# A two-layer hybrid decoder step: the samples' cache pages on three queues, groups of quarter products, and a wider operand in the compression

## Chip, core and metric

The kernel runs on one core of one Trainium2 chip. The metric is the device time of one launch in microseconds (us), the median of a few runs. One more execution was recorded by the hardware profiler; all rows below come from it.

## What is computed

A prompt of 512 tokens and 8 samples of one token each pass through two decoder layers with shared weights: half a feed-forward block, a token mixer of three branches (a state-space scan, sparse attention, a short convolution), half a feed-forward block, each followed by a layer norm. The change lies in the sparse attention of the samples. Each sample has 2048 past rows in 16 pages of 128 rows, found through a page table:

```python
def gather_pages(pool, layer, page_table):
    g = pool[layer, page_table]
...
past_cmp = gather_pages(past['cmp'], layer, past['page_table'])   # compression branch
past_sel = gather_pages(past['sel'], layer, past['page_table'])   # selection branch
...
h = jax.nn.gelu(h_a[:, :-1] + h_b[:, 1:] + h_pe)                  # nsa_compress: first layer
return h @ w2                                                     # second layer
...
kc = partial_rope(kc, c_end)
...
s_s = jnp.einsum('btkgd,btknsd->btkgns', qg, ks_sel)              # nsa_core: scores of the selected blocks
p_s = masked_softmax(s_s.reshape(flat), m_s.reshape(flat))
o_s = jnp.einsum('btkgm,btkmd->btkgd', p_s.astype(vsb.dtype), ...)
s_w = jnp.einsum('btkgd,bwkd->btkgw', qg, kw)                     # window branch
o = g[..., 0:1] * o_c + g[..., 1:2] * o_s + g[..., 2:3] * o_w
```

Compression turns every 32 raw rows into one key and one value by a two-layer network with a GELU; the scores on these choose 16 blocks of 64 rows; attention runs over the chosen blocks and over a window of 512 rows, and gates mix the three results.

## The kernel before

Within a layer the mixer's phases follow one another. During the layer norm ahead of the mixer and the projection of keys, values and queries (`project_kvq`, weights from `w_in`, loaded as `raw` by L218, split by ScalarE into `whi`, L228, and by VectorE into `wlo`, L229) the first pages are fetched. Then two strands are woven into one instruction stream per engine: `compress_cache` (the cached pages of the compression branch, sample by sample, `b` = 0 to 7) and `samples` (the attention of two samples at a time, group `g` = 0 to 3). The last group is woven with the prompt's own attention instead. Each strand is a generator that yields the length of its next wait; a planner picks which strand writes its next piece, and each engine executes what it was given strictly in that order.

The compression's first layer takes eight steps of 12 products per sample (L708, operand `xc`). ScalarE writes the operand's high part (L693, `xc` from `raw` or `cx`) and VectorE the low part (L694), two steps at a time lying ready: while TensorE multiplies one, the other is prepared. The second layer (`second`) takes the two GELUs from ScalarE (L730, `hc`), then four products with 64-column operands (L736: `w2` and the rotated `w2r`, for two key heads each, two instructions per product), two more for the values (L740), and VectorE applies the rotary factors.

A group's pages lie in four tiles `sg`, one for each sample `j` and each half `z` of its 16 pages: 8 pages of 128 KB in a tile, keys in the first 128 columns of a page, values in the others. `fetch_sel` fills them tile by tile: three pages (`NG` = 3) by an indirect transfer that GpSimd (POOL) issues (L1111), five by SyncE (SP), which reads the page numbers from the table into registers (TENSOR_LOAD, L628) and issues a transfer for each (L1115). The group's window rows follow on SP (L1120), then the next pages of the compression. The tiles have one set of buffers: the fetch for group g+1 starts when group g's last product with them (L1242) is done.

The products with pages are quarters: 32 output partitions each, one of TensorE's four column groups for each (z, j). Scores are made in two chunks `c` of four pages, four quarters each (L1182, two instructions per quarter, each 512 columns), in a PSUM bank `S`; then the window's scores (L1191) and those of the samples' own new keys (L1192). The values come in L1242 (pages), L1251 (window), L1255 to L1257 (own new rows and compressed values). The functions that the diff touches, and what calls them:

## Time and profile before

| | |
|---|---|
| median of 3 runs | 3113.18 us (3108.72 to 3114.4) |
| profiled execution | 3112.61 us |
| its span | 3110.9 us |
| mean granted TensorE clock | 0.987 of full speed |
| TensorE busy | 3037.4 us, 98% of the span |
| VectorE, ScalarE, GpSimd busy | 1599.5, 1121.8, 538.6 us |

The span is the stretch of the profiled execution from its first to its last instruction; the execution itself is 1.7 us longer. Busy shares are sums over the whole span. "PE" is TensorE's matmuls, "PEld" its weight loads, "DVE" VectorE, "ACT" ScalarE, "POOL" GpSimd, "SP" SyncE; a q behind an engine's name means its sequencer. The mixer with the samples' attention lies at about 490 to 700 us in the first layer and 2030 to 2245 us in the second.

### The profile page before, as it was taken

What the parts mean: (1) busy time and instruction counts of PE and PEld (TensorE: products, weight loads), DVE (VectorE), ACT (ScalarE), POOL (GpSimd) and SP (SyncE); (2) the same over time, 40 slices, a digit from 0 to 9 for tenths busy, and PEclk for the clock granted to TensorE, in tenths of its full rate; (3) what the DMA queues carried; (4) which work ended last, traced back from release to release, by engine and by line L of the source; (5) the groups of instructions that cost most, each with busy time, mean ns of one, the idle gap of its engine ahead of it and who ended that gap; (6) DMA issues with size and microseconds to landing.
All of it is one profiled execution on the core that took longest, in us unless ns stands there. A gap on an engine that the chain in (4) does not pass through costs nothing. (4 is left out here: it accounts for less than half of the span.)

```text
span 3110.9 us, 62132 instructions
## 1 busy us (share of the span) xinstructions
PE 3037.4 (98%) x25364; PEld 2908.1 (93%) x25364; DVE 1599.5 (51%) x3586; ACT 1121.8 (36%) x2226; POOL 538.6 (17%) x809
## 2 busy tenths in 40 slices
PE   8999999999999999999999999999999999999998
PEld 8999998777999999999999999886779999999998
DVE  7633356566655365333486334564666453743334
ACT  4332235466224233332233322354652342333322
POOL 2611031321001021001257011202210010210010
PEclk9999999999999999999999999999999999999999
DMA  5543254632553232232235332547234433223221
GB/s 158 200 149 128 89 158 137 213 96 59 155 138 105 82 109 82 82 109 85 92 102 171 91 102 89 159 124 216 83 88 134 130 98 97 95 82 100 91 86 64
DMA packets 358630, 360.17 MB, mean 116 GB/s; under 512 B 40068, under 2 KB 341668, under 8 KB 358216
## 3 DMA queue, kind: packets, MB, share of 16 engines
q1 hardware_dynamic: 342584, 333.58, 34.3%
q0 software_dynamic: 7440, 20.00, 2.2%
q8 instruction: 199, 3.26, 0.4%
q10 hardware_dynamic: 8320, 2.62, 0.4%
q14 instruction: 87, 0.71, 0.1%
HBM read 332.48 MB, written 36.28 MB: 119 GB/s over the span
## 5 line engine op out<-in xcount | busy, mean ns | idle before, releaser
L239 PE MATMUL ps<-xh,whi 128*128 128x264 f32 (+1 forms) x4448 | 1258.0, 286 | 14.4 <-ACT whi L228 6.9
L240 PE MATMUL ps<-xl,whi 128*128 128x264 f32 (+1 forms) x4448 | 1258.6, 284 | 2.0 <-DVE xl L323 2.0
L241 PE MATMUL ps<-xh,wlo 128*128 128x264 f32 (+1 forms) x4448 | 1254.8, 284 | 2.4 <-DVE wlo L229 2.4
L229 DVE TENSOR_TENSOR wlo<-raw,whi 128x1024 fp32r<-128x1024 f32 (+3 forms) x432 | 496.0, 1151 | 741.4 <-ACT whi L228 737.3
L239 PEld LDWEIGHTS ps<-xh,whi 128*128 128x128 f32 x4448 | 837.5, 189 | 19.0 <-ACT whi L228 7.7
L240 PEld LDWEIGHTS ps<-xl,whi 128*128 128x128 f32 x4448 | 840.0, 189 | 3.6 <-DVE xl L323 2.2
L241 PEld LDWEIGHTS ps<-xh,wlo 128*128 128x128 f32 x4448 | 839.3, 189 | 4.2 <-DVE wlo L229 3.6
L228 ACT ACTIVATE whi<-raw 128x1024 fp32r<-128x1024 f32 (+2 forms) x452 | 444.5, 988 | 888.4 <-PE ps L240 777.5
L240 PE MATMUL ps<-hl,whi 128*128 128x256 f32 (+1 forms) x1408 | 398.3, 283 | 0.0
L239 PE MATMUL ps<-hh,whi 128*128 128x256 f32 (+1 forms) x1408 | 398.2, 283 | 0.0
L241 PE MATMUL ps<-hh,wlo 128*128 128x256 f32 (+1 forms) x1408 | 398.1, 283 | 0.0
L241 PEld LDWEIGHTS ps<-hh,wlo 128*128 128x128 f32 x1408 | 265.3, 188 | 0.2
L239 PEld LDWEIGHTS ps<-hh,whi 128*128 128x128 f32 x1408 | 264.9, 188 | 0.3
L240 PEld LDWEIGHTS ps<-hl,whi 128*128 128x128 f32 x1408 | 264.8, 188 | 0.1
L260 POOL TENSOR_TENSOR xf<-xf,shift 128x264 f32<-128x264 f32 (+1 forms) x84 | 79.4, 981 | 1027.4 <-ACT shift L257 1027.4
L384 DVE TENSOR_TENSOR s<-s,ps 128x264 f32<-128x264 f32 (+1 forms) x176 | 74.3, 424 | 276.7 <-PE ps L241 276.3
L708 PE MATMUL ps<-xc,whi 128*128 128x256 f32 (+1 forms) x1024 | 166.2, 296 | 0.1
L385 ACT ACTIVATE hh<-s 128x264 fp32r<-128x264 f32 (+1 forms) x176 | 72.7, 415 | 245.1 <-DVE s L384 245.0
L708 PEld LDWEIGHTS ps<-xc,whi 128*128 128x128 f32 x1024 | 141.0, 191 | 14.9 <-issue 8.9
L1111 POOL DMA_INDIRECT sg<-in_selT_dram,idx x96 | 96.5, 1005 | 277.8 <-PE ps L1242 250.7
L382 ACT ACTIVATE s<-ps 128x264 f32<-128x264 f32 (+1 forms) x176 | 66.2, 378 | 128.0 <-PE ps L241 125.6
L386 DVE TENSOR_TENSOR hl<-s,hh 128x264 fp32r<-128x264 f32 (+1 forms) x176 | 76.2, 435 | 33.5 <-ACT hh L385 33.5
(471 smaller groups left out, 4216.3 us busy)
## 6 DMA issues: line engine op xcount, KB each, us to landing
raw<-in_ffn_w_gu_dram SPq DMA_DIRECT2D x86, 1024.0 KB
raw<-in_w_in_dram SPq DMA_DIRECT2D x38, 1024.0 KB
raw<-in_ffn_w_down_dram SPq DMA_DIRECT2D x32, 1024.0 KB
sg<-in_selT_dram SPq DMA_DIRECT2D x160, 128.0 KB
cx<-in_cmpT_dram SPq DMA_DIRECT2D x128, 128.0 KB
raw<-in_cmpT_dram SPq DMA_DIRECT2D x128, 128.0 KB
raw<-in_ffn_w_down_dram SPq DMA_DIRECT2D x16, 768.0 KB
W<-in_winT_dram SPq DMA_DIRECT2D x16, 512.0 KB
```

Source lines behind the costliest of these rows:

```text
L228: self.copy = self.nc.scalar.activation(hi, raw, AF.Copy)
L229: self.lo.tensor_sub(lo, raw, hi.bitcast(F32))
L239: nc.tensor.matmul(o, hi[:, k], rh, start=start and k == 0, stop=False)
L240: nc.tensor.matmul(o, hi[:, k], rl, start=False, stop=False)
L241: nc.tensor.matmul(o, lo[:, k], rh, start=False, stop=stop and k == nk - 1)
L260: nc.gpsimd.tensor_sub(self.xf[:, g, a:b], self.xf[:, g, a:b], sc[:, :n])
L382: nc.scalar.activation(s[:, :n], g, AF.Silu)
L384: nc.vector.tensor_mul(s[:, :n], s[:, :n], u)
L385: nc.scalar.activation(hh[:, j, a:b], s[:, :n], AF.Copy)
L386: nc.vector.tensor_sub(hl[:, j, a:b], s[:, :n], hh[:, j, a:b].bitcast(F32))
L708: nc.tensor.matmul(o, w[:, 2 * qq + q2, :], x[:, 2 * q2:2 * q2 + 2, z:z + n], start=not b and s < 2 and q2 + z + m == 0, stop=s > 5 and q2 ...
L1111: nc.gpsimd.indirect_dma_start(out=t[:, k], out_offset=None, in_=flat, in_offset=bass.IndirectOffsetOnAxis(ap=self.idx[:, l, b, z, k:k + 1 ...
```

## The change

`fetch_sel` works by halves: first the pages 0 to 3 of all four tiles, then the pages 4 to 7. Of four pages POOL fetches one by an indirect transfer (`NG` = 2, one for each half), ScalarE's queue one, and SP two. The page number of ScalarE's page is loaded into a register of ScalarE's. In `samples`, VectorE "opens" each bank by writing one column of zeros (`opened`), the window scores' four quarters stand together ahead of the two small products, and the last six value products are ordered so that both samples' stand side by side. The second layer of the compression takes one 128-column operand `w2k` (`w2` and its rotated copy side by side) for both key heads in one product of 256 columns (two instructions), and VectorE multiplies each head's half by itself.

```diff
-NG = 3
+NG = 2
...
-            nc.vector.tensor_copy(f, self.pt.rearrange("p b (z n) -> p b z n", z=2)[:, :, :, :NG])
+            nc.vector.tensor_copy(f, self.pt.rearrange("p b (z n) -> p b z n", z=2)[:, :, :, ::8 // NG])
...
-    def pages(self, src, l, b, p0, n):
+    def pages(self, src, l, b, p0, n, engine=mybir.EngineType.SP):
...
             pa = self.bank(self.ctp)
-            for j, w in enumerate((self.w2[:, 0], self.w2r)):
-                for kv in range(2):
-                    r = slice(kv * 64, kv * 64 + 64)
-                    nc.tensor.matmul(pa[r, j * 128:j * 128 + 128], w, h[:, kv, :], start=True, stop=True)
...
+            nc.tensor.matmul(pa[:, :256].rearrange("p (k n) -> p k n", k=2), self.w2k, h[:, 0:2, :], start=True, stop=True)
             for kv in range(2):
                 nc.tensor.matmul(pa[:, 256 + kv * 64:256 + kv * 64 + 64], h[:, 2 + kv, :], self.w2[:, 1], start=True, stop=True)
...
-            nc.vector.tensor_mul(t, pa[:, 128:256], self.C["kc_sin"])
-            nc.vector.tensor_mul(kcT, pa[:, :128], self.C["kc_cos"])
+            for kv in range(2):
+                r = slice(kv * 64, kv * 64 + 64)
+                nc.vector.tensor_mul(t[r], pa[64:128, kv * 128:kv * 128 + 128], self.C["kc_sin"][r])
+                nc.vector.tensor_mul(kcT[r], pa[0:64, kv * 128:kv * 128 + 128], self.C["kc_cos"][r])
...
         for z, j in which:
-            b, t = 2 * g + j, pg.tile([128, 8, 256], F32, name="sg")
-            G[z, j] = t
-            for k in range(NG):
+            G[z, j] = pg.tile([128, 8, 256], F32, name="sg")
+
+        for c in range(0, 8, 4):
+            for z, j in which:
+                b, t = 2 * g + j, G[z, j]
                 nc.gpsimd.indirect_dma_start(
-                    out=t[:, k], out_offset=None, in_=flat,
-                    in_offset=bass.IndirectOffsetOnAxis(ap=self.idx[:, l, b, z, k:k + 1], axis=0))
-            for k, s in enumerate(self.pages(src, l, b, 8 * z + NG, 8 - NG)):
-                nc.sync.dma_start(t[:, NG + k], s)
+                    out=t[:, c], out_offset=None, in_=flat,
+                    in_offset=bass.IndirectOffsetOnAxis(ap=self.idx[:, l, b, z, c // 4:c // 4 + 1], axis=0))
+                for e, k, n in ((mybir.EngineType.Activation, c + 1, 1), (mybir.EngineType.SP, c + 2, 2)):
+                    q = nc.scalar if n == 1 else nc.sync
+                    for i, s in enumerate(self.pages(src, l, b, 8 * z + k, n, e)):
+                        q.dma_start(t[:, k + i], s)
...
+    def opened(self, pool):
+
+        b = self.bank(pool)
+        self.nc.vector.memset(b[:, 0:1], 0.0)
+        return b
...
-            S = self.bank(self.saS)
+            S = self.opened(self.saS)
...
-        S = self.bank(self.saS)
+        S = self.opened(self.saS)
+        for z, j, r in quarters:
+            nc.tensor.matmul(S[r, :256], QB[:, 2 * g + j], G["w", j][:, 256 * z:256 * z + 256], start=True, stop=True)
         for j in range(2):
-            for z in range(2):
-                r = 64 * z + 32 * j
-                nc.tensor.matmul(S[r:r + 32, :256], QB[:, 2 * g + j], G["w", j][:, 256 * z:256 * z + 256], start=True, stop=True)
             nc.tensor.matmul(S[32 * j:32 * j + 32, 256:258], QB[:, 2 * g + j], self.kTs[:, :, 2 * g + j], start=True, stop=True)
...
         for j in range(2):
-            own, o = slice(32 * j, 32 * j + 32), slice(64 + 32 * j, 96 + 32 * j)
-            nc.tensor.matmul(O[own, :128], sT[:, own], self.srows[:, 128:256], start=False, stop=True, skip_group_check=True)
-            nc.tensor.matmul(O[own, 128:256], sT[:, o], self.srows[:, 384:512], start=False, stop=True, skip_group_check=True)
+            own = slice(32 * j, 32 * j + 32)
             nc.tensor.matmul(O[own, 256:384], pc[:, own], vc[:127, j], start=False, stop=True, skip_group_check=True)
+        for br in range(2):
+            for j in range(2):
+                own, o = (slice(k + 32 * j, k + 32 * j + 32) for k in (0, 64 * br))
+                nc.tensor.matmul(O[own, 128 * br:128 * br + 128], sT[:, o], self.srows[:, 256 * br + 128:256 * br + 256], start=False,
+                                 stop=True, skip_group_check=True)
```

The planner's order moves with it. Three places show how; names are tiles, and behind each row stand the semaphores that the instruction waits for (DMAHW and DMASW are transfers, an engine's name is that engine's work). A line of the file before up to L655 keeps its number; behind it the numbers grow by 1 to 13 (L693 is now L694, L708 L709, L730 L731, L1182 L1193, L1242 L1252, L1266 L1279).

The first place is ScalarE's order in the first layer, between groups 0 and 1, just behind the copy of the probabilities `PT` for group 0's last value products. Before, the rows of the compression's operand follow one another:

```order
L1227 ACTIVATE PT<-ps 128x512 [waits PE_49]
L693 ACTIVATE xc_5863<-raw 128x4x64 [waits DVE_49]
L693 ACTIVATE xc_5861<-raw 128x4x64 [waits DVE_49]
L1227 ACTIVATE PT<-ps 128x256 [waits PE_49]
L693 ACTIVATE xc_5861<-raw 128x4x64 [waits DVE_49]
L693 ACTIVATE xc_5863<-raw 128x4x64 [waits DVE_49,PE_49]
L693 ACTIVATE xc_5863<-raw 128x4x64 [waits DVE_49]
```

Now eight triples of a register load, an address computation (ISA) and a transfer stand between the copy and the next operand; these are the last three of them and what follows:

```order
L628 TENSOR_LOAD pt
L1120 ISA
L1120 DMA sg<-in_selT_dram 128x256 [waits DMAHW1_49]
L628 TENSOR_LOAD pt
L1120 ISA
L1120 DMA sg<-in_selT_dram 128x256 [waits DMAHW3_49]
L628 TENSOR_LOAD pt
L1120 ISA
L1120 DMA sg<-in_selT_dram 128x256 [waits DMAHW5_49]
L694 ACTIVATE xc_5884<-raw 128x4x64 [waits DVE_49,PE_49]
L694 ACTIVATE xc_5884<-raw 128x4x64 [waits DVE_49]
```

The writes of `xc` (`xc_5884` now, `xc_5863` before) that stood directly behind the copy now stand behind the eight pages; the first four of these transfers wait for TensorE's last use of their tile. The same block of eight stands between groups 1 and 2 and between groups 2 and 3, in both layers. Ahead of group 0 the eight stand singly among the norm's writes (L322).

The second place is TensorE's order at the same point of the program, from the last value products of group 0 on. Before:

```order
L1257 MATMUL ps<-vc,pc 32x128
L708 MATMUL ps<-xc_5861,whi 128x256 [waits Activation_49]
L708 MATMUL ps<-xc_5861,whi 128x256 x3
L708 MATMUL ps<-xc_5861,wlo 128x256 x4
L708 MATMUL ps<-xc_5862,whi 128x256 [waits DVE_49]
L708 MATMUL ps<-xc_5862,whi 128x256 x3
L708 MATMUL ps<-xc_5863,whi 128x256 [waits Activation_49]
L708 MATMUL ps<-xc_5863,whi 128x256 x3
L708 MATMUL ps<-xc_5863,wlo 128x256 x4
L708 MATMUL ps<-xc_5864,whi 128x256 [waits DVE_49]
L708 MATMUL ps<-xc_5864,whi 128x256 x3
L1266 MATMUL ps<-cst,OS 128x64 [waits DVE_49]
```

Now:

```order
L1265 MATMUL ps<-vc,pc 32x128 x2
L1269 MATMUL ps<-srows,sT 32x128 [waits DVE_49]
L1269 MATMUL ps<-srows,sT 32x128 x3
L709 MATMUL ps<-xc_5882,whi 128x256 x4
L709 MATMUL ps<-xc_5882,wlo 128x256 x4
L709 MATMUL ps<-xc_5883,whi 128x256 [waits DVE_49]
L709 MATMUL ps<-xc_5883,whi 128x256 x3
L1279 MATMUL ps<-cst,OS 128x64 [waits DVE_49]
L1193 MATMUL ps<-sg,QB 32x512 [waits DMAHW2_49,DMAHW7_49,DMAHW0_49,DMASW5_49]
L709 MATMUL ps<-xc_5884,whi 128x256 [waits Activation_49]
L709 MATMUL ps<-xc_5884,whi 128x256 x3
```

One step of 12 products instead of two stands ahead of the group's last transposition (L1279, before L1266), the first quarter of the next group follows it, and the next step waits for the `xc` that ScalarE writes behind its pages.

The third place is where TensorE takes the other quarters of group 1. Before, they stand with a lone first quarter ahead of them, and mixed with the previous softmax's small products:

```order
L1182 MATMUL ps<-sg,QB 32x512 [waits DMASW3_49,DMAHW3_49,DMASW2_49,DMASW1_49]
L1142 MATMUL ps<-cst,scp 127x4 [waits DVE_49,Activation_49]
L1143 MATMUL ps<-cst,scp 127x64
L1182 MATMUL ps<-sg,QB 32x512 [waits DMASW6_49,DMAHW0_49,DMASW5_49,DMASW4_49]
L1182 MATMUL ps<-sg,QB 32x512 [waits DMASW7_49,DMAHW5_49,DMASW1_49,DMASW0_49]
L1182 MATMUL ps<-sg,QB 32x512 [waits DMASW4_49,DMAHW2_49,DMASW3_49,DMASW2_49]
L1182 MATMUL ps<-sg,QB 32x512 [waits DMAHW7_49,DMAHW6_49,DMAHW4_49]
L1151 MATMUL ps<-cst,pt 33x33 [waits Activation_49]
L1151 MATMUL ps<-cst,pt 33x33 x3
L1182 MATMUL ps<-sg,QB 32x512 [waits DMAHW4_49,DMAHW3_49,DMAHW1_49]
L1182 MATMUL ps<-sg,QB 32x512 [waits DMAHW6_49,DMAHW7_49,DMAHW1_49,DMAHW0_49]
L1182 MATMUL ps<-sg,QB 32x512 [waits DMAHW5_49,DMAHW6_49,DMAHW4_49,DMAHW3_49]
```

Now seven quarters stand nearly together, 72 products of L709 behind the first one:

```order
L709 MATMUL ps<-xc_5883,whi 128x256 x3
L1193 MATMUL ps<-sg,QB 32x512 [waits DMAHW4_49,DMAHW6_49,DMAHW1_49,DMASW6_49]
L1193 MATMUL ps<-sg,QB 32x512 [waits DMAHW2_49,DMAHW3_49,DMAHW0_49,DMASW7_49]
L1193 MATMUL ps<-sg,QB 32x512 [waits DMAHW5_49,DMAHW6_49,DMAHW4_49,DMASW0_49]
L1193 MATMUL ps<-sg,QB 32x512 [waits DMAHW7_49,DMAHW0_49,DMASW1_49]
L1153 MATMUL ps<-cst,scp 127x4 [waits DVE_49,Activation_49]
L1154 MATMUL ps<-cst,scp 127x64
L1193 MATMUL ps<-sg,QB 32x512 [waits DMAHW2_49,DMAHW1_49,DMASW2_49]
L1193 MATMUL ps<-sg,QB 32x512 [waits DMAHW4_49,DMAHW3_49,DMASW3_49]
L1193 MATMUL ps<-sg,QB 32x512 [waits DMAHW6_49,DMAHW5_49,DMASW4_49]
```

A quarter still waits for three or four transfers of its own tile, now for one of ScalarE's, two of SP's and one of POOL's. 

## Rows read from the trace of the kernel before

**Rows 1.** Profile page, part 1: busy time, share of the span, instructions.
```profile
PE 3037.4 (98%) x25364; PEld 2908.1 (93%) x25364; DVE 1599.5 (51%) x3586; ACT 1121.8 (36%) x2226; POOL 538.6 (17%) x809
```

**Rows 2.** TensorE's waits, second layer's mixer: total us, times, longest.
```profile
PE ps L1182 <- DMA sg<-in_selT_dram,idx: 4.6, 2, 2.9
PE ps L239 <- ACT whi L228: 3.6, 1, 3.6
```

**Rows 3.** TensorE's timeline: group 1's quarters, first layer (start, length, line, tiles).
```profile
571.79 1.04 PE L1182 MATMUL ps<-sg,QB 128*32 128x512 f32 x2
572.76 0.38 PE L1142 MATMUL ps<-cst,scp 64*127 64x4 f32 x2
...
573.23 1.05 PE L1182 MATMUL ps<-sg,QB 128*32 128x512 f32 x4
576.15 1.14 PE L1182 MATMUL ps<-sg,QB 128*32 128x512 f32 x4 [1.86 <-DMA raw<-in_cmpT_dram]
577.22 0.45 PE L1151 MATMUL ps<-cst,pt 127*33 127x33 f32 x8
577.60 1.06 PE L1182 MATMUL ps<-sg,QB 128*32 128x512 f32 x6
578.59 0.39 PE L708 MATMUL ps<-xc,whi 128*128 128x256 f32 x1
```

**Rows 4.** TensorE's timeline: group 2's quarters, second layer, first and last row.
```profile
2161.92 1.05 PE L1182 MATMUL ps<-sg,QB 128*32 128x512 f32 x2
...
2170.10 0.39 PE L708 MATMUL ps<-xc,whi 128*128 128x256 f32 x1
```

**Rows 5.** TensorE's timeline: group 3's eight quarters together, first layer.
```profile
669.48 1.92 PE L1182 MATMUL ps<-sg,QB 128*32 128x512 f32 x16
```

**Rows 6.** TensorE's timeline behind group 0's last page product, first layer.
```profile
554.99 0.74 PE L708 MATMUL ps<-xc,whi 128*128 128x256 f32 x4
...
557.20 0.40 PE L1255 MATMUL ps<-srows,sT 8*32 8x128 f32 x2
...
558.97 0.39 PE L708 MATMUL ps<-xc,whi 128*128 128x256 f32 x1
```

**Rows 7.** TensorE's timeline: the second layer of sample 3's compression, first layer.
```profile
563.69 0.88 PE L708 MATMUL ps<-xc,whi 128*128 128x256 f32 x6
564.51 0.44 PE L736 MATMUL ps<-hc,w 128*64 128x128 f32 x4
...
565.09 0.66 PE L740 MATMUL ps<-w,hc 128*128 128x64 f32 x4
```

**Rows 8.** Sequencer instructions by line (min/median/max ns); two pages on SP's timeline.
```profile
L628 SPq TENSOR_LOAD <-pt x64: 522/972/1087, 409.8 to 2202.0; - x64
...
L1560 ACTq DMA_DIRECT2D du<-U x8: 366/366/628, 780.0 to 2444.8; - x8
...
452.76 0.85 SPq L1115 DMA_DIRECT2D sg<-in_selT_dram  x2
```

**Rows 9.** Busy by stretch (PE, PEld, DVE, ACT, POOL, PEclk, DMA share, GB/s).
```profile
563.00:567.00 4.00, 4.00 (x36) 3.58 (x35) 1.59 (x5) 2.58 (x6) 3.09 (x3) 1.00 0.90 283
...
575.00:579.00 4.00, 2.85 (x21) 1.16 (x22) 1.06 (x6) 0.00 (x0) 0.00 (x0) 1.00 0.92 315
```

**Rows 10.** ScalarE's timeline, groups 0 to 1 and 2 to 3, first layer.
```profile
556.25 0.72 ACT L693 ACTIVATE xc<-raw 128x256 fp32r<-128x256 f32 x2 [2.35 <-PE ps L708]
...
643.91 0.72 ACT L693 ACTIVATE xc<-raw 128x256 fp32r<-128x256 f32 x2 [1.92 <-PE ps L708]
...
649.55 0.63 ACT L967 ACTIVATE raw<-qT 64x512 fp32r<-64x512 f32 x1
```

**Rows 11.** TensorE's timeline: the compression's second layer, last sample, first layer.
```profile
652.01 0.44 PE L736 MATMUL ps<-hc,w 128*64 128x128 f32 x4 [0.84 <-ACT hc L730]
```

**Rows 12.** Busy by stretch around the wait for `w_in`, second layer.
```profile
2000.00:2002.30 2.30, 0.15 (x2) 0.00 (x0) 0.00 (x0) 0.00 (x0) 0.00 (x0) 1.00 0.81 230
2002.30:2009.20 6.90, 4.97 (x21) 4.67 (x22) 5.44 (x12) 3.19 (x6) 0.00 (x0) 0.51 0.05 10
```

More of the change, by code (lines that the diff above doesn't have):

```diff
@@ L516, in mid @@
         self.w2 = a.tile([128, 2, 64], F32, name="w2")
-        self.w2r = a.tile([128, 64], F32, name="w2r")
+        self.w2k = a.tile([128, 128], F32, name="w2k")
         self.hpe = a.tile([128, 2], F32, name="hpe")
@@ L624, in page_rows @@
                 nc.vector.tensor_scalar(self.idx[:, l], f, float(l * NPOOL * 128), None, op0=OP.add)
-    def pages(self, src, l, b, p0, n):
+    def pages(self, src, l, b, p0, n, engine=mybir.EngineType.SP):
         _, vs = self.nc.values_load_multi_w_load_instructions(
-            self.pt[0:1, b, p0:p0 + n], engines=[mybir.EngineType.SP], min_val=0, max_val=NPOOL - 1,
+            self.pt[0:1, b, p0:p0 + n], engines=[engine], min_val=0, max_val=NPOOL - 1,
             skip_runtime_bounds_check_because="the table holds page numbers of the pool")
@@ L658, in compress_start @@
             self.lo = nc.vector
-        nc.vector.memset(self.w2r, 0.0)
-        nc.vector.tensor_scalar(self.w2r[:, 0:8], self.w2[:, 0, 8:16], -1.0, None, op0=OP.mult)
-        nc.vector.tensor_copy(self.w2r[:, 8:16], self.w2[:, 0, 0:8])
+        nc.vector.memset(self.w2k[:, 64:], 0.0)
+        nc.vector.tensor_copy(self.w2k[:, 0:64], self.w2[:, 0])
+        nc.vector.tensor_scalar(self.w2k[:, 64:72], self.w2[:, 0, 8:16], -1.0, None, op0=OP.mult)
+        nc.vector.tensor_copy(self.w2k[:, 72:80], self.w2[:, 0, 0:8])
         return p, pet
@@ L732, in second @@
             pa = self.bank(self.ctp)
-            for j, w in enumerate((self.w2[:, 0], self.w2r)):
-                for kv in range(2):
-                    r = slice(kv * 64, kv * 64 + 64)
-                    nc.tensor.matmul(pa[r, j * 128:j * 128 + 128], w, h[:, kv, :], start=True, stop=True)
-                    if b == 0:
-                        nc.tensor.matmul(pa[r, 384 + j * 32:416 + j * 32], w, hp[0][:, 0, kv], start=True, stop=True)
+            nc.tensor.matmul(pa[:, :256].rearrange("p (k n) -> p k n", k=2), self.w2k, h[:, 0:2, :], start=True, stop=True)
             for kv in range(2):
                 nc.tensor.matmul(pa[:, 256 + kv * 64:256 + kv * 64 + 64], h[:, 2 + kv, :], self.w2[:, 1], start=True, stop=True)
+            if b == 0:
+                nc.tensor.matmul(pa[:, 384:448].rearrange("p (k n) -> p k n", k=2), self.w2k, hp[0][:, 0], start=True, stop=True)
             t = p.tile([128, 128], F32, name="kct")
-            nc.vector.tensor_mul(t, pa[:, 128:256], self.C["kc_sin"])
-            nc.vector.tensor_mul(kcT, pa[:, :128], self.C["kc_cos"])
+            for kv in range(2):
+                r = slice(kv * 64, kv * 64 + 64)
+                nc.vector.tensor_mul(t[r], pa[64:128, kv * 128:kv * 128 + 128], self.C["kc_sin"][r])
+                nc.vector.tensor_mul(kcT[r], pa[0:64, kv * 128:kv * 128 + 128], self.C["kc_cos"][r])
             nc.vector.tensor_add(kcT, kcT, t)
@@ L747, in second @@
                 t = p0.tile([128, 32], F32, name="pt1")
-                nc.vector.tensor_mul(t, pa[:, 416:448], self.C["kc_sin"][:, :32])
                 nc.gpsimd.memset(self.kcp, 0.0)
@@ L751, in second @@
                     r = slice(kv * 64, kv * 64 + 64)
-                    nc.vector.tensor_mul(self.kcp[r, kv], pa[r, 384:416], self.C["kc_cos"][r, :32])
+                    nc.vector.tensor_mul(t[r], pa[64:128, 384 + kv * 32:416 + kv * 32], self.C["kc_sin"][r, :32])
+                    nc.vector.tensor_mul(self.kcp[r, kv], pa[0:64, 384 + kv * 32:416 + kv * 32], self.C["kc_cos"][r, :32])
                     nc.vector.tensor_add(self.kcp[r, kv], self.kcp[r, kv], t[r])
@@ L1127, in samples @@
         QB, kcT, vc = self.QB, self.kcT, self.vc
-        M = self.bank(self.saM)
+        M = self.opened(self.saM)
         for j in range(2):
@@ L1237, in samples @@
         yield 300.0
-        O = self.bank(self.saS)
+        O = self.opened(self.saS)
         for c in range(8):
```

## Prediction

> **What bounds the kernel now.** The profile page comes first: TensorE is busy for 3037 of 3110.9 us [rows 1], so what counts is TensorE's own work and its few idle stretches, and a transfer or a ScalarE write only where TensorE stands for it. Next I read TensorE's waits in the mixer. Of those that the change touches, the quarter products wait for pages, 4.6 us in two waits in the second layer, and the projection waits 3.6 us for the split weights of `w_in` [rows 2]. The timeline shows that the waits for pages are only the visible part. Group 1's quarters in the first layer begin at 571.79, and the stretch is over at 578.59: 6.80 us [rows 3], though a lone quarter takes 0.97 (571.79 to 572.76), and the small products between take 0.47 (572.76 to 573.23) and 0.38 (577.22 to 577.60). Eight quarters whose pages are all there take 1.92 [rows 5]. So half the stretch is waiting. The same stretch is 8.18 us long for group 2 in the second layer [rows 4]; four such stretches (groups 1 and 2, both layers: 6.80, 5.99, 8.70 and 8.18) sum to 29.7 us. [...]
>
> **The change part by part**, against the profiled 3112.6 us (the median of the runs is 0.6 above).
>
> Quarters. If the pages are there, a stretch becomes 0.97 for the first quarter, 0.85 of small products and at most 1.92 for the other seven: 3.74, four times 15.0, so −14.7 us. Whether they are there: a fetch moves 32 pages of 128 KB, 4.2 MB, which at the 283 GB/s of the window needs 14.8 us; the DMA engines are then at 0.90 [rows 9], so no way of issuing makes it much shorter. SP's share falls from 20 pages to 16. Now the seven quarters come behind 72 products, at about 19 to 20 us after the tiles are free, and the first quarter needs only half a tile. I leave 0.5 us of waiting each, +2 (bounds 0 and the 3.0 of now each).
>
> Value products. The twelve instructions of L1255 to L1257 take 1.77 us, 557.20 to 558.97 [rows 6], first sample 0's three products on one column group, then sample 1's. Side by side the two take the time of one, 0.89, as quarters on different column groups do [rows 3, 5]. Eight groups: −7.1.
>
> Second layer. L736 takes 0.58 us, 564.51 to 565.09 [rows 7]. The new product has two instructions of 256 columns; a lone quarter's two of 512 take 0.97 [rows 3], so 0.49. Sixteen samples: −1.6. It waits for the first GELU only; of the six waits like the 0.84 [rows 11] I take −1 (0 to −2). VectorE's two more operations per sample and the 40 writes of `opened` are hidden: VectorE is busy for 51% [rows 1]. Were they not, 40 of some 0.1 us would be 4 us. The window scores were already overlapping; nothing.
>
> The weights of `w_in`. Their load stands on SP behind the first fetch. Before, this costs SP four loads of 0.97 and twenty pages 0.52 apart (0.85 less 0.33 for two), 14.3 us; now eight loads of 0.52 (the shortest; a load of two numbers is not in the trace) and sixteen pages, 12.5 [rows 8]. The load starts some 2 us earlier in both layers, with fewer pages under way. I take −4 (0, if the transfer itself is late, to −9, if the 3.4 us of slow clock go too [rows 12]).
>
> ScalarE's pages. This is the disputed cost. The trace has no register load on ScalarE. From SP's rows a page needs 0.52 for its load, 0.37 for the transfer's issue (ScalarE's own row, L1560) and 0.18 around it, the rest of SP's spacing of 0.52 [rows 8]: 1.07. The first load is done before the tile is free, so eight pages hold ScalarE for 8 × 0.55 + 7 × 0.52 = 8.0 us. Queued behind is the next `xc`, which before was written at 556.25, 1.3 us after the tiles came free at 554.99 [rows 6, 10]. Half of its 0.72 must be there, so TensorE gets it at 563.4. What TensorE has until then, by the new order: the rest of a step and the window's value products (2.21, 554.99 to 557.20, less two products that now stand earlier, 0.2), the six value products 0.89, one prepared step of twelve (six take 0.82 [rows 7]: 1.6), the transposition and one quarter 0.97; some 5.6 us. It is through at 560.6 and stands for 2.8 us: groups 0 to 1 and 1 to 2, both layers, 4 × 2.8 = +11.
>
> Between groups 2 and 3 no quarter fills, and the stall is 3.8. Then the last GELU: before, eight copies of 0.63 (L966, L967) stand ahead of it; now three, but 6.7 us of pages beyond the 1.3, so it comes 6.7 − 5 × 0.65 = 3.4 us later than the wait that ended at 652.01 [rows 10, 11], and the five others lie behind it, in front of the prompt's softmax. I take 4.5 each, +9.
>
> Bounds for both: if the load costs nothing on ScalarE, the page is 0.55, eight take 4.4, `xc` is there at 559.8 and TensorE never stands; if each load takes the median 0.97, it is 11.2 and the stall 6.0. I take 0.52, since these loads read one number.
>
> Clock. Six stalls of 3 to 4 us are new. The 3.6 at 2000 brought 6.9 us of slow clock [rows 12], the 1.86 at 576 none [rows 9]. Between these I let three of six bring half of that cost, 1.7: +5 (0 to 20); the slow stretch behind the second layer's page waits goes: −1.
>
> First fetch. Eight pages now stand singly among ScalarE's writes of the norm, where TensorE is close behind: 1 us per layer, +2 (0 to 6). In group 0 three more quarters run apart from the others: 2 × 0.97, +1.9.
>
> The sum: −14.7 + 2 − 7.1 − 1.6 − 1 − 4 + 11 + 9 + 5 − 1 + 2 + 1.9 = +1.5, so about 3114 us. The gains and ScalarE's stalls cancel.
>
> **The rivals.**
>
> Slower, by the clock: every one of the six stalls of ScalarE brings the full slow stretch of 6.9 us. Six times 3.4 instead of 5 makes +15: 3129 us. It decides from stalls of about 3 us on; for it speaks the 3.6 [rows 2, 12], against it the 1.86 [rows 9]. Loads of 0.97 would bring nearly the same by themselves, 4 × 3.2 + 2 × 4 = +21: 3135.
>
> Slower, because the pages come no earlier: the DMA share of 0.90 and 0.92 during the fetch [rows 9] says that the engines, not the queues, hold the pages back, and W's and the compression's transfers follow close behind. Then the seven quarters still wait some 2.5 us each, +10 less the 2 counted: 3122. [...]
>
> Faster, since ScalarE's issue is cheap: a page of 0.55. The stalls and their clock go, 11 + 9 + 5: 3089 us. For it, that a sequencer may load while the engine works; against it, that SP's own loads stand in its line one after the other.
>
> Faster by the rest: the issue costs as reckoned, but no stall slows the clock, the wait for `w_in` goes with its slow stretch (−9) and the norm hides the first fetch: −5 − 5 − 2, some 3102.
>
> **How the numbers follow.** A measurement here can tell 0.2%, 6 us. The forecast, 3114, with its own range from 3107 to 3119: 0.36. Slower by clock or loads 0.24, by late pages 0.10; cheap issue 0.18; the rest 0.12. So faster 0.30, same 0.36, slower 0.34. The range leaves out the ends of the two outer rivals: 3094 to 3134.
>
> **What would show it.** In the profile of the changed kernel: register loads on ScalarE of about 0.52 us and pages 1.07 apart; eight of them behind L1237; TensorE waiting some 3 us for `xc` (L694) at L709 in each of the six places; the quarters L1193 with hardly any wait for transfers; L1265 to L1269 in 0.9 us; the load of `w_in` 2 us earlier. The prediction is wrong if the pages are less than 0.8 or more than 1.4 apart, if the clock falls behind every stall or none, or if ScalarE is late in the prompt's attention by more than the 4.5 us.

## The result and the profile after

The changed kernel takes 3135.17 us (median of 7 runs, 3128.56 to 3138.37), the kernel before beside it 3114.4 (7 runs, 3108.7 to 3124.25). The ratio is 1.0064, with an interval from 1.0053 to 1.0074: slower by 21 us, where the prediction said no change that can be told. The profiled execution took 3135.51 us. First the page, part 1 (before: [rows 1]).

```profile
PE 3035.7 (97%) x25256; PEld 2916.8 (93%) x25256; DVE 1616.2 (52%) x3662; ACT 1122.0 (36%) x2226; POOL 508.8 (16%) x777
```

TensorE is busy for 1.7 us less, in a span that is 22.7 us longer. What it waits for has changed; this is the view of its waits over the whole span (total us, times, longest).

```profile
PE ps L709 <- ACT xc L694: 20.1, 6, 4.9
...
PE ps L735 <- ACT hc L731: 4.8, 4, 1.2
PE ps L1026 <- DVE cP L1022: 3.7, 4, 1.6
...
PE ps L1049 <- DVE cP L1014: 3.0, 2, 1.6
```

The first row is new: the compression stands six times for `xc`, which ScalarE writes. Page waits [rows 2] are down to two of 1.3 and 1.2 us, both at the first quarter of group 1, and the projection no longer waits for `w_in`. TensorE's timeline in the place of [rows 3] and [rows 6] shows what was gained there:

```profile
557.67 0.39 PE L1265 MATMUL ps<-vc,pc 127*32 127x128 f32 x4
558.00 0.63 PE L1269 MATMUL ps<-srows,sT 8*32 8x128 f32 x8
558.55 0.74 PE L709 MATMUL ps<-xc,whi 128*128 128x256 f32 x4
...
561.75 1.02 PE L1193 MATMUL ps<-sg,QB 128*32 128x512 f32 x2 [1.33 <-DMA sg<-in_selT_dram]
...
565.34 1.22 PE L709 MATMUL ps<-xc,whi 128*128 128x256 f32 x4 [2.57 <-ACT xc L694]
...
577.59 1.06 PE L1193 MATMUL ps<-sg,QB 128*32 128x512 f32 x8
578.59 0.38 PE L1153 MATMUL ps<-cst,scp 64*127 64x4 f32 x2
579.06 1.06 PE L1193 MATMUL ps<-sg,QB 128*32 128x512 f32 x6
580.05 0.74 PE L709 MATMUL ps<-xc,whi 128*128 128x256 f32 x4
```

The value products take 0.88 us instead of 1.77; the other seven quarters run without a wait, here and in the three other such places. The price is the 2.57 for `xc`. Nearly all that is lost, though, lies in one stretch of each layer: from group 2's last transposition (L1266 before, L1279 after) to group 3's. It takes in the page fetch for group 3, the last compression, the start of the prompt's attention and group 3's scores. Here it is in both layers, first before, then after (start and end; PE, PEld, DVE, ACT, POOL, granted clock, DMA share, GB/s):

```profile
649.60:698.40 48.80, 45.40 (x400) 33.21 (x398) 33.07 (x111) 28.72 (x93) 13.00 (x17) 0.93 0.29 87
2197.70:2245.70 48.00, 44.41 (x399) 32.18 (x397) 32.94 (x111) 28.66 (x93) 13.01 (x17) 0.96 0.31 92
```

```profile
649.80:712.90 63.10, 53.04 (x406) 41.02 (x404) 37.88 (x123) 34.09 (x102) 10.31 (x15) 0.78 0.23 74
2207.90:2270.90 63.00, 51.44 (x405) 39.35 (x403) 37.84 (x123) 34.15 (x102) 10.32 (x15) 0.81 0.23 75
```

The stretch is 14.3 us longer in the first layer and 15.0 in the second, and the clock in it falls from 0.93 and 0.96 to 0.78 and 0.81. Set against the span's difference of 22.7: the projections are 1.9 and 4.9 shorter; group 0 to group 2 together +2.1 in the first layer and −4.4 in the second; the rest of the layers +4.6 and −2.1.

In each stretch the loss is of two kinds in about equal parts. In the first layer TensorE is busy for 7.6 us more (53.04 against 45.40) with about as many products (406 and 400), and stands for 6.7 more; in the second layer it is 7.0 and 8.0.

ScalarE's timeline shows how the stretch starts; the eight pages that ScalarE issues are the row ACTq.

```profile
643.88 0.72 ACT L694 ACTIVATE xc<-raw 128x256 fp32r<-128x256 f32 x2 [1.48 <-PE ps L709]
645.34 8.75 ACTq L1120 DMA_DIRECT2D sg<-in_selT_dram  x8
654.19 0.72 ACT L694 ACTIVATE xc<-raw 128x256 fp32r<-128x256 f32 x2 [9.59 <-DMA sg<-in_selT_dram,idx]
...
657.11 1.28 ACT L731 ACT_TABLE_LOAD   x1
658.41 0.83 ACT L731 ACTIVATE hc<-ps,hpe 128x254 f32<-128x254 f32 x2
...
665.01 0.36 ACT L1147 ACTIVATE scp<-ps,scm 64x127 f32<-64x127 f32 x1
```

Before, the last `xc` stood at 643.91 [rows 10] and, in the same view, that GELU at 651.49 and the softmax's first exponential at 655.47. The GELU and the exponential are now 6.9 and 9.5 us later. TensorE stands 4.86 us for `xc` and then runs at 0.50 of full speed, as the windows after that wait show:

```profile
650.00:657.00 7.00, 2.14 (x10) 2.04 (x10) 2.31 (x7) 2.52 (x5) 4.05 (x5) 0.77 1.02 329
657.00:664.00 7.00, 7.00 (x33) 6.06 (x31) 3.97 (x10) 5.91 (x11) 0.00 (x0) 0.50 0.84 272
664.00:671.00 7.00, 4.78 (x22) 4.00 (x21) 6.08 (x25) 4.57 (x18) 0.00 (x0) 0.50 0.05 19
671.00:678.00 7.00, 6.81 (x45) 5.18 (x44) 4.47 (x20) 3.01 (x13) 1.04 (x1) 0.77 0.00 0
```

Between 664 and 671 further waits fall into the slow time, and the clock comes back only within the last window, some 20 us after it fell. Before, one slow stretch of 6.8 us lay here. A second one follows in the changed kernel, 694.6 to 701.4 at 0.51; the second layer's stretch has three, of 6.8, 6.8 and 10.2 us.

### The profile page after: what moved, and what is told of

The parts are those of the page before. It is cut to its first block, busy times and chain, and to the rows that moved or that the text cites. A ratio compares the mean times of both kernels' runs of the same rounds, so it can differ in the third digit from the quotient of the medians.

```text
span 3133.6 us, 62123 instructions
## 1 busy us (share of the span) xinstructions
PE 3035.7 (97%) x25256; PEld 2916.8 (93%) x25256; DVE 1616.2 (52%) x3662; ACT 1122.0 (36%) x2226; POOL 508.8 (16%) x777
## 5 line engine op out<-in xcount | busy, mean ns | idle before, releaser
L709 PE MATMUL ps<-xc,whi 128*128 128x256 f32 (+1 forms) x1024 | 173.0, 304 | 24.2 <-ACT xc L694 20.1
L709 PEld LDWEIGHTS ps<-xc,whi 128*128 128x128 f32 x1024 | 146.7, 198 | 40.3 <-ACT xc L694 25.4
L1114 POOL DMA_INDIRECT sg<-in_selT_dram,idx x64 | 61.8, 966 | 292.8 <-PE ps L1252 205.1
```

The source lines that it names most:

```text
L709: nc.tensor.matmul(o, w[:, 2 * qq + q2, :], x[:, 2 * q2:2 * q2 + 2, z:z + n], start=not b and s < 2 and q2 + z + m == 0, stop=s > 5 and q2 ...
L1114: nc.gpsimd.indirect_dma_start(out=t[:, c], out_offset=None, in_=flat, in_offset=bass.IndirectOffsetOnAxis(ap=self.idx[:, l, b, z, c // 4: ...
```

## The experiments

The runs were spread over several chips and fall into two kinds. On kind A the kernel before takes 3111 to 3118 us, as beside the first measurement of the change; on kind B it takes 3204 to 3209, and the changed kernel 3179 (what differs there is in the last section). A ratio holds for its kind alone; the kind is named with each run.

**Pages on SP, kind B.** ScalarE's page of each half is issued by SP.

```diff
-                for e, k, n in ((mybir.EngineType.Activation, c + 1, 1), (mybir.EngineType.SP, c + 2, 2)):
...
+                for e, k, n in ((mybir.EngineType.SP, c + 1, 3),):
...
```

> The changed kernel with ScalarE's page given to SP (one page by POOL, three by SP, in each half of each tile); all else as changed. Theory A (ScalarE's queue is held by its pages, TensorE waits behind it for the compression's operand and the GELU, and the slow clock follows): the three waits of L709 for xc in each layer go, the stretch from group 2's end to the prompt's attention (+14.5 and +15 us against before) shrinks by at least 12 us per layer, total 3092 to 3102 us; quarters may wait up to 2 us per group again. Theory B (the loss is the new order and VectorE's extra work, not the queue): 3128 to 3136 us, the prompt's stretch as long as in the changed kernel.

Measured: 3205.25 against 3208.09, ratio 0.999 (0.998 to 0.9999).

**Old fetch, kind B.** `fetch_sel` and `NG` of the kernel before, with the rest of the change.

```diff
-NG = 2
+NG = 3
...
-                for e, k, n in ((mybir.EngineType.Activation, c + 1, 1), (mybir.EngineType.SP, c + 2, 2)):
...
+            for k, s in enumerate(self.pages(src, l, b, 8 * z + NG, 8 - NG)):
+                nc.sync.dma_start(t[:, NG + k], s)
```

> The changed kernel with the fetch of before (tile by tile, three pages by POOL, five by SP); opened banks, order of the products and the wide operand stay. Theory A: the remaining parts are worth 7 to 12 us, the quarters wait for pages as before, total 3101 to 3108 us. Theory B: the remaining parts are what costs, 3120 to 3136 us.

Measured: 3225.45, 1.0054 (1.0037 to 1.007).

**ScalarE not in group 3, kind B.** As the first, for group 3's fetch alone.

```diff
-                for e, k, n in ((mybir.EngineType.Activation, c + 1, 1), (mybir.EngineType.SP, c + 2, 2)):
+                for e, k, n in (((mybir.EngineType.SP, c + 1, 3),) if g == 3 else ((mybir.EngineType.Activation, c + 1, 1), (mybir.EngineType.SP, c + 2, 2))):
```

> The changed kernel, but group 3's fetch (the one that stands ahead of the prompt's attention) without ScalarE (one page by POOL, three by SP); ScalarE's pages stay for groups 0 to 2. Theory A as refined by the trace (nearly all of the loss is the prompt's stretch, 14.5 to 15 us per layer; between groups 0 to 2 gains and stalls cancel): 3104 to 3110 us. Rival C (each stall costs alike, a third of the loss lies at each of the three fetches): 3118 to 3126 us. Theory B: 3128 to 3136 us.

Measured: 3173.99, 0.990 (0.9883 to 0.9916).

**ScalarE in the first half only, kind B.** As the first, for each tile's second half (`if c`) alone. 

> The changed kernel, ScalarE fetching one page per tile in the first half only (four instead of eight per fetch), SP three pages in the second half. Theory A: the block on ScalarE is 3.7 instead of 8 to 8.8 us, xc is there before TensorE has used up its work, so the waits of L709 for xc fall under 1 us each and the total is 3094 to 3105 us. If instead any page on ScalarE costs because of its place ahead of xc (half the pages, half the loss): 3113 to 3120 us.

Measured: 3175.16, 0.9894 (0.9878 to 0.9911).

**The changed kernel, kind B.** No edit. 

> The changed kernel itself, to have it beside the others on the same chip, since the four runs before were made on a chip on which the kernel before took 3208 us. If the chip runs as the first one did: ratio to the kernel before 1.0064 (3135 against 3114 us). If it runs as the second one: the ratio tells how the changed kernel stands there, by theory A above e5's 0.990.

Measured: 3179.15 against 3204.57, 0.9916 (0.99 to 0.9933).

**The first four again, kind B.** Pages on SP, beside the changed kernel: 

> As e1 (ScalarE's page given to SP). On a chip like the first, theory A: 3092 to 3102 us, ratio 0.993 to 0.996, no wait of L709 for ScalarE's xc; theory B (order and VectorE's extra work are what costs): ratio 1.004 to 1.007.

And once more: 

> The changed kernel with ScalarE's page given to SP (one page by POOL, three by SP, in each half), now that the kernel before takes 3114 us again. Theory A (ScalarE's queue is held by its eight pages, TensorE stands behind for xc and the GELU, the slow clock follows): no wait of L709 for ScalarE's xc, the stretch from group 2's last transposition to group 3's falls from 63 to 50 us or less in both layers, 3092 to 3102 us in all (ratio 0.993 to 0.996). Theory B (the new order and VectorE's extra work cost): ratio 1.004 to 1.007.

Measured: 3202.7 (0.9994) and 3204.51 (1.0001). Old fetch: 

> As e4 (the fetch of before, everything else changed). On a chip like the first, theory A: ratio 0.996 to 0.999, waits for pages as before; theory B: 1.002 to 1.007.

And: 

> The changed kernel with the fetch of before; the opened banks, the order of the products and the wide operand stay. Theory A: waits for pages as before, the rest worth 7 to 12 us: ratio 0.996 to 0.998. Theory B: 1.002 to 1.007.

Measured: 3222.98 (1.0063) and 3219.81 (1.0049). ScalarE not in group 3: 

> As e5 (group 3's fetch without ScalarE). On a chip like the first, theory A: ratio 0.996 to 0.999, since the prompt's stretch loses its 14.5 and 15 us; rival C (each fetch's stall costs alike): 1.001 to 1.004.

And: 

> ScalarE's pages for groups 0 to 2 only, group 3's by POOL and SP. Theory A as the two traces size it (14.5 and 15 us of the loss in the prompt's stretch, gains and stalls cancelling elsewhere): ratio 0.996 to 0.999. Rival C (each fetch's stall costs alike): 1.001 to 1.004.

Measured: 3174.31 (0.9905) and 3172.4 (0.9902). ScalarE in the first half only: 

> ScalarE fetches one page per tile in the first half only, four instead of eight per fetch. Theory A: the block is 3.7 us instead of 8 to 8.8, xc is there in time, waits of L709 for xc under 1 us: ratio 0.993 to 0.998. If any page ahead of xc costs (half the pages, half the loss): 1.000 to 1.003.

Measured: 3173.95 (0.9911). All repeat within 0.2%. So on kind B the change is a gain of 0.8%, on kind A a loss of 0.6%, and the four runs above can't explain the loss. Against the changed kernel on kind B all pages on SP lose 24 us; the 5 us that ScalarE out of group 3 seems to gain lie within the two intervals (0.9905, 0.9889 to 0.9922, beside 0.9916, 0.99 to 0.9933). What the old fetch does show there is that the other parts by themselves are no gain: with them alone the kernel is 15 to 18 us above the kernel before, in theory B's range each time.

**The kernel before by itself, kind A.** No edit. 

> The kernel before, unchanged, for its trace on this chip. If it takes about 3205 us here as in the two sessions before, its trace should show where the 90 us above the first trace lie: by what the traces of e1, e4 and r0 show, in the six stretches in which pages are fetched, with every engine's sequencer slow (some 0.7 us for an instruction that takes 0.03 otherwise) while POOL's indirect transfers run, 12 to 16 us per fetch. If instead it takes 3113 us, the chip is like the first one, and ratios to it can be read as such.

Measured: 3114.05, with 3112.3 us of span and a clock of 0.987, about as before (3110.9 and 0.987).

**Pages on SP, kind A.** The first edit again. 

> The changed kernel with ScalarE's page given to SP, run alone beside the kernel before, as the first measurement was (in the three sessions with four kernels the kernel before took 3205 us, alone 3114). Theory A (ScalarE's queue is held by its eight pages): no wait of L709 for ScalarE's xc, the stretch from group 2's last transposition to group 3's falls from 63 to 50 us or less, 3092 to 3102 us, ratio 0.993 to 0.996. Theory B (the new order and VectorE's extra work cost): ratio 1.004 to 1.007.

Measured: 3156.66 against 3117.81, 1.0122 (1.0095 to 1.015). TensorE's waits in this kernel:

```profile
PE ps L239 <- ACT whi L228: 15.5, 5, 7.1
...
PE ps L1193 <- DMA sg<-in_selT_dram: 6.1, 3, 2.2
```

Neither theory had this time. With all of ScalarE's pages on SP the six waits for `xc` behind ScalarE's pages are gone (two are left in the second layer, 3.3 us together, in which ScalarE itself waits for the compression's pages), and something dearer takes their place: 24 pages stand in SP's queue ahead of the raw `w_in`, so the projection waits, 5.3 and 7.1 us of the 15.5, and the pages are late again. Some 8.5 of the 45.4 us by which this span is longer than that of the kernel before already stand ahead of the mixer, in the first feed-forward block; why is not known. The stretch to group 3's transposition is 56.6 and 55.5, halfway back.

**ScalarE not in group 3, kind A.** The third edit again. 

> ScalarE's pages for groups 0 to 2 only, alone beside the kernel before. Up to group 2 its order is that of the changed kernel, so the stretches ahead keep their times. Stretch from group 2's last transposition (L1279) to group 3's: 63 us in both layers of the changed kernel, 48.8 and 48.0 before. Theory A (the pages on ScalarE's queue): back to 48 to 51 us, total 3104 to 3110 us. Theory B (the new order of ScalarE's copies, L967 and L968 behind the GELU, and VectorE's extra work): 60 to 63 us, total 3130 to 3136. Half and half, as the run with all pages on SP suggests (56.6 and 55.6 us there): 55 to 58 us, total 3118 to 3124.

Measured: 3120.23 against 3112.54, 1.0024 (1.0012 to 1.0036). The stretch in this kernel, both layers:

```profile
652.00:707.50 55.50, 48.97 (x391) 37.51 (x391) 34.58 (x118) 29.80 (x95) 9.80 (x14) 0.82 0.26 79
2202.80:2256.80 54.00, 46.41 (x392) 35.18 (x392) 34.47 (x118) 29.69 (x95) 9.77 (x14) 0.87 0.29 83
```

This is the expectation's half and half. ScalarE's eight pages of group 3 are worth 7.6 and 9.0 us, with the clock that falls behind them. Another 6.7 and 6.0 us are lost though ScalarE now is in time. Its timeline of TensorE shows longer waits there than before, in the first layer (before: none at the first of these places, 0.33 and 0.15 at the others):

```profile
653.85 0.38 PE L1142 MATMUL ps<-kcT,QB 128*32 128x127 f32 x2 [0.82 <-DVE ps L1131]
...
688.58 0.22 PE L1241 MATMUL ps<-cst,ex 64*8 64x64 f32 x1 [0.69 <-DVE ex L1224]
...
693.03 0.69 PE L1026 MATMUL ps<-cst,cP 128*128 128x128 f32 x2 [2.05 <-DVE cP L1022]
```

The first is the write of `opened`, and the same kernel's timeline of VectorE says why a write of 0.06 us holds TensorE for 0.82:

```profile
652.58 0.34 DVE L1282 COPY ysam<-ps 64x8 f32<-64x8 f32 x2
652.95 0.68 DVE L969 TENSOR_TENSOR raw<-qT,raw 64x512 fp32r<-64x512 f32 x1
653.64 0.06 DVE L1131 MEMSET ps<- 128x1 f32 x1
653.74 0.68 DVE L970 TENSOR_TENSOR raw<-qT,raw 64x512 fp32r<-64x512 f32 x1
```

VectorE is behind with the rotation of the queries, one operation of 0.68 after the other, and the write stands in that line. In the changed kernel itself no wait of TensorE ends with one of the 40 writes.

The wait at `cP` (L1026) is there in the changed kernel too, 1.63 us in the first layer and 1.45 in the second, and its trace shows what made it, first before, then after:

```profile
682.94 0.17 DVE L1020 TENSOR_TENSOR cm<-cm,gtok 128x8 f32<-128x8 f32 x1
683.02 0.68 DVE L1095 TENSOR_TENSOR pw<-pw,ps 128x512 f32<-128x512 f32 x1
```

```profile
695.29 0.68 DVE L1096 TENSOR_TENSOR pw<-pw,ps 128x512 f32<-128x512 f32 x1
696.12 1.27 POOL L1097 TENSOR_TENSOR yb<-yb,pw 128x512 f32<-128x512 f32 x1 [6.26 <-DVE cm L1019]
696.29 1.12 DVE L1021 TENSOR_TENSOR cm<-cm,gtok 128x8 f32<-128x8 f32 x1
```

VectorE's order has changed: the small product with the gates (L1020, now L1021), on the way to `cP`, now stands behind the large one (L1096), which sets GpSimd's product going, and beside that it takes 1.12 us instead of 0.17. It is so in both layers, and in the kernel with ScalarE out of group 3; with the new fetch alone (below) the old order stands, and the wait is 0.3 at most.

**Old fetch, alone, kind B.** The second edit again. 

> The changed kernel with the pages of a fetch issued as before: three by GpSimd and five by SP for a half tile set, none by ScalarE. The other parts (opened banks, order of the value products, wide second-layer operand) stay. It runs alone beside the kernel before. Theory C (the 6 to 7 us per layer that stay lost behind the last compression when ScalarE has no pages there come from those other parts and the order of work that they lead to): the stretch from group 2's to group 3's last transposition stays at 54 to 56 us, the value products and the second layer are shorter by about 5 us per layer elsewhere, the page waits are back, and the time is 3118 to 3126. Theory D (they come from the fetch too, since the pages of groups 0 to 2 move the work of the prompt): the stretch goes back to 48 to 50 us, and with the shorter products the time is 3098 to 3108.

Measured: 3221.53 against 3209.39, 1.0036 (1.0025 to 1.0047). It was meant for kind A and fell on B; the stretch is 56.2 and 56.0 there, with no trace of the kernel before on that kind to hold it against. It decides between neither theory; the time is again 12 us above the kernel before. So the question was turned round:

**The new fetch only, kind A.** The kernel before with `fetch_sel`, `pages` and `NG` of the changed one; banks, order of the value products and second layer as before.

```diff
-NG = 3
+NG = 2
...
-            for k, s in enumerate(self.pages(src, l, b, 8 * z + NG, 8 - NG)):
-                nc.sync.dma_start(t[:, NG + k], s)
+                for e, k, n in ((mybir.EngineType.Activation, c + 1, 1), (mybir.EngineType.SP, c + 2, 2)):
+                    q = nc.scalar if n == 1 else nc.sync
...
```

> The kernel before with the new fetch alone (two pages of a half by SP, one by ScalarE, one by GpSimd); banks, order of the value products and the second layer stay as before. Measured alone beside the kernel before. Theory C (behind the last compression the fetch costs what ScalarE's pages take, 7.6 and 9 us, and the other 6 to 7 us of that stretch come from the other parts of the change): the stretch from group 2's to group 3's last transposition is 55 to 58 us, the value products and the second layer lose their 5 us per layer again, and the time is 3126 to 3134, close to the changed kernel's. Theory D (the fetch alone leads to the whole 14 to 15 us): the stretch is 61 to 65 us and the time 3142 to 3150, above the changed kernel's, since the shorter products are missing.

Measured: 3121.44 against 3110.89, 1.003 (1.0019 to 1.0042). The stretch in this kernel, both layers:

```profile
646.30:702.60 56.30, 50.84 (x411) 37.85 (x409) 36.51 (x116) 33.91 (x102) 9.77 (x14) 0.85 0.26 80
2197.10:2255.60 58.50, 51.73 (x412) 38.78 (x410) 36.54 (x116) 33.97 (x102) 9.66 (x14) 0.82 0.26 79
```

Theory C for the stretch (the second layer half a microsecond above its range), and better than either in time. The fetch alone costs 7.5 and 10.5 us in the stretch and gives some back up to group 2: its last transposition is 3.3 us earlier than before in the first layer, and in the second 9.8 earlier once the 9.2 us that the layer begins late are taken off. The other parts of the change are then no gain at all: with them the kernel goes from 1.0030 to 1.0064, and the intervals lie apart. The stretches of four kernels agree with two causes that add:

| from group 2's to group 3's last transposition, us | layer 1 | layer 2 |
|---|---|---|
| kernel before | 48.8 | 48.0 |
| new fetch only | 56.3 (+7.5) | 58.5 (+10.5) |
| changed, ScalarE not in group 3 | 55.5 (+6.7) | 54.0 (+6.0) |
| changed | 63.1 (+14.3) | 63.0 (+15.0) |

7.5 + 6.7 make 14.2 of 14.3; 10.5 + 6.0 make 16.5 of 15.0.

**The new fetch only, ScalarE not in group 3, kind B.** The edit before, with `if g == 3` of the third. 

> The kernel before with the new fetch alone, and in group 3's fetch ScalarE's page issued by SP; banks, value products and second layer as before. Theory (the costs of the changed kernel add up from two places: 7.5 and 9 to 10 us per layer of ScalarE's pages in the stretch behind the last compression, and the rest from the other parts): without both, that stretch is 48 to 51 us in both layers and the time 3100 to 3108, below the kernel before's 3111. Rival (the fetch moves the last compression's copies on ScalarE by itself, as in the changed kernel with ScalarE not in group 3, where the stretch was 55.5 and 54.0): the stretch stays at 53 to 56 and the time is 3110 to 3116.

Measured: 3165.63 against 3204.8, 0.9875 (0.9856 to 0.9895). The shortest time on kind B, 14 us below the changed kernel; the 8 below the changed one without ScalarE in group 3 lie within the intervals. The stretch is 51.7 and 51.6, where the changed kernel shows 60.2 and 58.7 on that kind: both causes out, 8.5 and 7.1 us gone. It lies between the theory's 48 to 51 and the rival's 53 to 56, nearer the theory, and with no trace of the kernel before on this kind it can't be said what was left. On kind A it was not run. If the ratios there combine as the stretches do, 1.0030 + 1.0024 − 1.0064 make 0.999; that would be an estimate of no change, not a gain.

## Why the prediction was wrong

**The step that failed** lies in the stretch between groups 2 and 3, in two terms. For both layers the forecast had there 9 us for ScalarE's pages ("I take 4.5 each, +9"), at most 3.4 for the clock (two of its three stalls at 1.7), and nothing for the other parts ("hidden: VectorE is busy for 51%"): 12.4. The stretches cost +14.3 and +15.0, so 29.3. ScalarE's pages of group 3, with the clock behind them, are 16.6 of this (7.6 + 9.0): place and mechanism were named, the size was 4 us short. The larger miss is the term at nothing: the other parts cost there 11.3 us on top of the new fetch (63.1 less 56.3, 63.0 less 58.5), and 12.7 are left when ScalarE is out of group 3 (6.7 + 6.0). All the rest was to bring −10.9 and brings −6.6. What was undersized:

- The delay of ScalarE. Reckoned: the last GELU 3.4 us later; measured 6.9, and the exponential after it 9.5. Of the 3.5 beyond the reckoning 2.6 are that the tiles come free later: the first page of group 3 is issued at 645.34 instead of 642.74, since in the new order group 2's last page products stand one step of the compression later (644.24 instead of 641.65). Another 0.75 is the length of the block, 8.75 instead of 8.0: in it one page waited 1.9 us, from 649.82 to 651.72, for an earlier page of the block to land, whose semaphore it shares (the last four pages of this block wait so for the first four). Neither was in a term.
- The clock. The term let a stall bring half of what the slow stretch in [rows 12] costs: 6.90 us at 0.51 are 3.4 us of full clock lost, half of it 1.7. Behind the 4.86 us the slow time lasted 20 us; the waits for `scp` and `cP` lie in it, though that they prolong it is not shown. A second slow stretch follows in the first layer, and in the second layer there are three. Granted 0.78 of 63.1 us instead of 0.93 of 48.8 is 13.9 us of full clock lost instead of 3.4, but part of this fell where TensorE stood anyway: by its busy time the clock can have cost no more than 7.6 and 7.0 us of the 14.3 and 15.0.
- What was costed at nothing. The busy share was the wrong cover. In this stretch VectorE works on the chain (rotations, scores, `cP`), and what moves in its order is waited for: the 1.63 and 1.45 us at `cP` are such a wait, with a slow stretch of 6.8 and 10.2 us around it, where the new fetch alone waits 0.3 at most. The bound that the text gave, 4 us, was for the writes alone. How much of the 11 us each of the three parts has (the writes, the product order, the wide operand), and how much the order that the planner then chose, was not taken apart; a wait for a write, 0.82 us, is shown only in the kernels without ScalarE in group 3.

**What was right.** Page waits: the quarters run without waits, but for the two of 1.3 and 1.2 us, as the −14.7 + 2 had it, and the trace doesn't bear the rival of late pages out: the pages come early enough. ScalarE's stall helps in this: SP issues group 1's last page at 571.17, pages of SP's land a median of 3.7 us after their issue, and the seven quarters begin at 577.59, behind the 2.57 us for `xc`; whether they would wait without it is not shown. The value products: 0.88 us, forecast 0.89. `w_in`: 1.9 and 4.9 us, forecast −4 with the first fetch's +2 against it. ScalarE's pages: 0.94 us apart instead of 1.07, as the load takes 0.28 us there and not the 0.52 taken from SP, and the blocks of the first layer 8.56, 7.76 and 8.75 us instead of 8.0. That the blocks come so near is in part luck: at 0.94 a page they would be some 7.1 (0.55 and seven times 0.94), and waits, most of them for earlier pages to land, fill the rest. The sequencer rows by line (min/median/max ns):

```profile
L628 SPq TENSOR_LOAD <-pt x96: 462/473/877, 409.9 to 2216.6; - x96
L628 ACTq TENSOR_LOAD <-pt x64: 272/278/472, 405.8 to 2210.2; - x64
```

The stalls between groups 0 to 1 and 1 to 2: 2.6, 2.9, 1.7 and 3.4 us, four that sum to 10.6 where +11 was forecast. The clock term holds for these four: behind three of them the clock is low for 3.4 us (1.7 lost, as forecast), behind the 1.7 it stays at 1.00. "Cheap issue", at 0.55 a page, fell, though 18 of ScalarE's 64 loads ran beside one of its own operations, as at 643.88.

Two rivals came nearer in time than the forecast, and neither describes the run. "Slower, by the clock" (3129) had 6.9 us of low clock behind each of the six stalls; behind one there is none, behind three 3.4, and 27 and 24 us in the two stretches of the other two. The 3135 for loads of 0.97 us is the measured time by luck, as the loads took 0.28. In the sum, 16 times 0.09 for the second layer is −1.4 and not −1.6; nothing hangs on it.

**What the sum hid.** A gain ahead of a stall is no gain. With the new fetch only, TensorE's wait at this line is

```profile
PE ps L708 <- ACT xc L693: 13.3, 6, 3.9
```

against 20.1 in the changed kernel: the value products save 0.9 in each of six places, and TensorE stands 1.1 longer in each. The prediction had both −7.1 and the stalls, each right by itself, and reckoned the stalls with the shorter products, so its sum is not wrong in this; but as long as ScalarE ends the wait, the first only feeds the second.

## What to carry to other kernels

Work that moves to an engine's queue should be priced where that engine is on the chain, stage by stage: the same eight pages bring stalls of 1.7 to 3.4 us, with at most 3.4 us of low clock behind each, where TensorE has a compression to run, and cost 7.6 and 9.0 where GELU, softmax and a longer time of low clock come behind them. A busy share over the whole kernel doesn't say that small added operations are hidden; look at the engine's timeline in the stage where TensorE waits for it, and at what stands in a new order there. And before adding up a gain and a stall at the same place, ask which of them ends the wait.

## What the runs showed of the hardware

For one kernel there were two kinds of chips, or of conditions of a chip: the kernel before took 3111 to 3118 us five times (kind A) and 3204 to 3209 five other times (kind B). On kind B TensorE waits during the page fetches; this is the first row of its waits, of the changed kernel there:

```profile
PE ps L1279 <- DVE OS L1277: 47.5, 6, 10.0
```

VectorE, for which it waits, stands still itself. Its timeline in the last experiment, behind group 0's values in the first layer:

```profile
554.56 0.06 DVE L1181 MEMSET SB<- 64x2 f32 x1
566.85 0.35 DVE L1266 TENSOR_SCALAR OS<-ps,cf 128x128 f32<-128x128 f32 x1 [12.23 <-remote]
```

The products that L1266 reads ended at 559; nothing on this core releases it in the trace. The MOVE ahead of a page, with a median of 0.03 us, took up to 0.71 on SP with all pages there, and up to 0.70 on ScalarE with ScalarE not in group 3, both on kind B; in the two traces of the first measurement, on kind A, it never took more than 0.03. The wait for `OS` does not stand among TensorE's waits in these two. The cause was not found. It goes with how the pages are fetched: TensorE's waits for `OS` sum to 47.5 us in the changed kernel, 38.0 in the last experiment, 24.5 with the old fetch alone and 8.8 with all pages on SP (in these last two TensorE stands for 40.1 and 21.6 us at the compression's L709 instead, with nothing in the trace that it waits for).

The granted clock after one wait of 4.86 us, with further waits in the time behind it, stayed at 0.50 of full speed for about 20 us; behind the second layer's 4.75 us, and behind the wait of 3.6 us in [rows 12], it stayed there for 6.8 and 6.9 us, and behind 2.57 us for 3.4.

VectorE's product of 128x8 with the gates stands eight times in the kernel before and eight times in the changed one: it took 0.15 to 0.17 us in the ten places where no GpSimd product ran beside it, and 0.99 to 1.12 in the six where one of 1.26 or 1.27 us did.
